# A transformer trunk in fp32: a written engine order for the mixing stages, and the sibling's order behind mixing and in the last output

## The chip, the cores and the metric

The kernel runs on one core of one Trainium2 chip. A core has TensorE (PE, with its weight loads shown apart as PEld), VectorE (DVE), ScalarE (ACT), GpSimd (POOL) and SyncE (SP), each with an instruction queue of its own that it works off in order; 16 DMA engines move data, on requests that here come from SP and POOL. The metric is device time in microseconds (us) of one execution, the median of several.

## The reference, cut to what matters

Two layers over 512 tokens of width 1024. Each layer is a half-step SwiGLU feed-forward, a mixing step, and a second feed-forward; each is preceded by an RMS norm with a scale and shift made from `c`.

```python
for l in range(DEPTH):
    mod = (c_act @ w_ada[l] + b_ada[l]).reshape(B, N_MOD, D_MODEL)
    hn = rms_norm(h, g_ffn1[l]) * (1.0 + sc1) + sh1
    h = h + 0.5 * (1.0 + gt1) * swiglu(hn, w_ffn1_in[l], w_ffn1_out[l])
    hn = rms_norm(h, g_mix[l]) * (1.0 + sc2) + sh2
    proj = hn @ w_mix_in[l]
    y_att = sliding_window_sink_attention(p_att, ...)   # 8 heads of 64, window 128
    y_rwkv = rwkv7_time_mix(p_rwkv, ...)                # 4 heads of 64, a recurrence over time
    y_conv = short_conv_mix(p_conv, conv_w[l])
    h = h + (1.0 + gt2) * (concatenate([y_att, y_rwkv, y_conv]) @ w_mix_out[l])
    hn = rms_norm(h, g_ffn2[l]) * (1.0 + sc3) + sh3
    h = h + 0.5 * (1.0 + gt3) * swiglu(hn, w_ffn2_in[l], w_ffn2_out[l])
```

## The kernel before

Activations lie transposed, 128 channels on the partitions and 512 tokens along the free axis. Large products are made in float32 accuracy from three products of reduced words: ScalarE casts a weight tile to its high half `wH` (`split`, L145), VectorE subtracts it to get the low half `wL` (L147), and `mm3` (L133 to L135) issues high x high, high x low and low x high. Weight tiles of 128 x 1024 arrive in `wraw` (two buffers); `wH` and `wL` have four buffers each. The feed-forwards make part of their products by a Strassen scheme with fewer block products (`prod`, L440 to L442, sums of weights by accumulating DMAs and by VectorE).

PSUM banks go by four tags, `mm`, `r0`, `r1` and `x`, two buffers each. `psmm` turns through the tags it is given with a counter, `turn`.

*Norms.* `norm` gives five steps. While the last two output tiles (6 and 7) of a stage are still being made in halves of 256 tokens, `stats` sums the squares over channels with tiny products into `ps_ss` (L279), takes root and reciprocal, `spread` turns the result across partitions by PE, and `apply` writes the normed `hn` as high and low parts (L296 to L298). The squares of tiles 0 to 6 are added on VectorE into `ss` (L255); that of tile 7, and of tile 6 in mixing, goes to `stats` apart.

*Projections.* `projector` makes the tiles of a stage's first product. Where it begins on its own, the first three tiles are made side by side in halves of the tokens, so that PE can start when the first half of `hn` is there; further tiles follow one by one, each with the next weights fetched ahead.

*Mixing* (`mix`). Twenty projection tiles feed three coroutines: `rwkv` (the recurrence in chunks of 64, many small products in 64 x 64 tiles), `attention` (scores, softmax, transposes `ps_pt`, averages `ps_av`) and `inverse` (a triangular inverse on VectorE that goes twice through DRAM on POOL's queue). A loop places their steps between the large products with a hand-kept clock (`STEP`, `PACE`, `DELAYS`, `WAITS`, `HALFWAY`). Order edges hold a step behind the large product ahead of it (`pe`, L808 to L814) and a few pairs of instructions apart. Beyond those edges a scheduler orders each engine's instructions when the program is built; on the chip the order on each engine is fixed. Names that the text uses: `lo`, `ps_w`, `ps_a` (decay and rate from a low-rank product), `rn`, `rk`, `rs` (sums for roots, 32 tiny products each), `ps_vt` (turn of the values `vr`), `ps_q`, `ps_rq` (norm of the queries), `ps_c`, `ps_x`, `ps_t`, `ps_gn`, `ps_o`, `ps_s`, `ps_ys` (the recurrence), `yr` (its result). Then six output tiles, and tiles 6 and 7 in halves.

*The last output* (`strassen_out`). The last feed-forward's second group has no norm behind it. For u = 0 and 1 it makes four output tiles each by products into `ps_d`, `ps_f`, `ps_g`; for u = 0, `rest_rows` also makes the part of all eight tiles that does not fit the scheme, through tag `x`, with its own weight tile each four.

Of the kernel before, what the change touches and what calls it, by code (L numbers as in the profile page):

```python
# [17 lines left out]
P = 128  # L18
# [30 lines left out]
WAITS = (5, 5, 4)  # L49
HALFWAY = (2.5, 2.5)  # L50
LOG = False


# [21 lines left out]
def trunk_kernel(ctx, tc, ins, out, layers=L, phases=("ffn1", "mix", "ffn2")):  # L75
# [52 lines left out]

    def mm3(acc, w, k, x, sl, start, stop):

        wH, wL, xH, xL = w[0][:, k], w[1][:, k], weave(x[0][:, sl]), weave(x[1][:, sl])
        acc = paired(acc)
        mm(acc, wH, xH, start=start, stop=False)  # L133
        mm(acc, wH, xL, start=False, stop=False)  # L134
        latest["large"] = mm(acc, wL, xH, start=False, stop=stop)  # L135

    latest = {}

    def queue_behind(name):
        return tc.issue_after(latest[name].ins) if name in latest else nullcontext()  # L140

# [105 lines left out]
    def add_ss(ss, i, sl=ALL):  # L247

        if ss is None:
            return  # L250
        if i == 0:
            act(ss[:, sl], h[0][:, sl], AF.Square)
        else:
            sq = square(i, sl)
            latest["dve"] = tt(ss[:, sl], ss[:, sl], sq, ALU.add)  # L255

# [5 lines left out]
    def norm(l, g, ish, isc, ss):  # L262

        hn = [tuple(hnp[k // 4].tile([P, T], F32R, name=n, tag="hn") for n in ("hnH", "hnL")) for k in range(KD)]
        gm = small_.tile([P, KD], F32, name="gmod", tag="gmod")
        rstd = {}

        def scale(ks=slice(0, KD)):
            stt(gm[:, ks], mod[l, isc][:, ks], 1.0, prm(l, g)[:, ks], ALU.add, ALU.mult)

        def stats(sl, sqs):

            pt = psum([P, 2], "ps_ss")
# [8 lines left out]
            latest["dve"] = nc.vector.reciprocal(r, r)  # L282
            rstd[sl.start] = r

        def spread(sl):

            r, pt = rstd[sl.start], psum([P, T // 2], "ps_rstd", "r0" if sl.start else "x")
            for b in range(2):
                mm(pt[:, b * P : (b + 1) * P], r[:, b : b + 1].to_broadcast([P, P]), cst("ident"), start=True, stop=True, is_transpose=True)
            rstd[sl.start] = pt  # L290

        def apply(sl, ks=range(KD)):
            for i in ks:
                a, b, sh = hn[i][0][:, sl], hn[i][1][:, sl], mod[l, ish][:, i : i + 1]
# [3 lines left out]
                latest["dve"] = latest["norm_dve"] = stt(b, t, sh, a.bitcast(F32), ALU.add, ALU.subtract)  # L298

        return hn, scale, stats, spread, apply  # L300


    loads = []

# [9 lines left out]
    def projector(srcs, hn, tags, pts=None, ahead=0, ready=(), first=("mm", "mm", "r1")):  # L314


        ws = list(ready) if pts is None else [None] * len(pts) + list(ready)

        def fetch(n):

            places = {3: ("norm_act", "norm_dve"), 4: ("act", "dve")} if ready and pts is None else {}
            ws.extend(load_w(s, behind=places.get(len(ws))) for s in srcs[len(ws) : n])

        if pts is None:
            fetch(3)
            pts = [psum([P, T], "ps_mm", tag) for tag in first]
            for sl in HALVES:
                for k in range(KD):
                    for w, pt in zip(ws, pts):
                        mm3(pt[:, sl], w, k, hn[k], sl, k == 0 and sl is HALVES[0], k == KD - 1 and sl is HALVES[1])  # L330
                    yield
            whole = [Woven(pt, 2) for pt in pts]
        else:
            whole = [Woven(pt) for pt in pts]
        n0 = len(pts)
        fetch(n0 + ahead)
        yield from whole
        for n in range(n0, len(srcs)):
            fetch(n + 1 + ahead)
            w = ws[n]  # L340
            pt = psmm(tags)
            for k in range(KD):
                mm3(pt, w, k, hn[k], ALL, k == 0, k == KD - 1)
                yield
            yield Woven(pt)

    def residual(pt, i, gate, ss, sl=ALL):
        hs = inorder(h[i][:, sl])
        done = stt(hs, Woven(pt).view, gate[:, i : i + 1], hs, ALU.mult, ALU.add)  # L349
        add_ss(ss, i, sl)  # L350
        return done
# [6 lines left out]
    def ffn(l, w_in, w_pair, w_out, hn, im, ss, need, then, first, ready, coming):  # L358
# [6 lines left out]
        with tc.tile_pool(name="act", bufs=1) as ap_:  # L365
# [10 lines left out]
            def hl(w, add_to=None):  # L376
                pair = tuple(wp.tile([P, KD, P], F32R, name=x, tag=x, bufs=4) for x in ("wH", "wL"))
                parted = split(*pair, w)
# [148 lines left out]
            def strassen_out(j0, j1):  # L527
# [37 lines left out]

                def rest_rows(u):
                    w = hl(raw_([(slice(2 * i, 2 * i + 2), w_out[l, 4 * u + i, :, kc:j1]) for i in range(4)]))
# [5 lines left out]
                    return classical  # L573

                for u in range(2):
                    tags = ("mm", "r0", "r1") if u else ("mm", "r1", "r0")
# [175 lines left out]

    def mix(l, hn, ss, mp, then, ready):
        wi, wo1, wo2 = ins["wmi"], ins["wmo1"], ins["wmo2"]

# [52 lines left out]
        def pe(*args, **kw):  # L808

            m = mm(*args, **kw)  # L810
            if lead[0] is not None:
                tc.add_manual_dep(m.ins, lead[0].ins.name, ORDER, reason="a step stands behind the large products before it")
                lead[0] = None
            return m  # L814
# [242 lines left out]
        def rwkv():  # L1057
# [91 lines left out]
            def invert():  # L1149
# [8 lines left out]
                for lev in range(2):  # L1158
# [7 lines left out]
                    for later in held if lev else ():  # L1166
                        tc.add_manual_dep(later.ins, new.ins.name, ORDER, reason="the inverse goes first")
                    yield 1.4, 3.2
# [165 lines left out]
        def attention():  # L1334
# [44 lines left out]
            def together(m, other, kind=ORDER):  # L1379

                if other is not None:
                    tc.add_manual_dep(m.ins, other.ins.name, kind, reason="both groups run together")

# [13 lines left out]
            for b in range(NB):  # L1397
# [4 lines left out]
                for g, (Sc, (den, es)) in enumerate(zip(both, dens)):  # L1402
# [4 lines left out]
                    for later in turns if (b, g) == (2, 0) else ():  # L1407
                        tc.add_manual_dep(later.ins, share.ins.name, ORDER, reason="shares go first")
                    yield 0, 1.4
# [73 lines left out]
        spread(HALVES[1])  # L1483
        apply(HALVES[1])


    what = {"ffn1": ("g1", 0), "mix": ("gm", 3), "ffn2": ("g2", 6)}
# [171 lines left out]
    for n, (l, p) in enumerate(seq):  # L1659
# [111 lines left out]
```

## Time and profile before

| | |
|---|---|
| median of 3 runs | 1773.5 us (1771.95 to 1773.51) |
| profiled execution | 1774.42 us |
| its span, first to last instruction | 1772.7 us |
| first mixing stage | from about 358 to 572 us |
| second mixing stage | from about 1231 to 1447 us |
| last output | from about 1718 us |

The page gives busy time, instructions and share of the span of each engine. In the timeline a row has the start, the length from first start to last end, engine, line, operation, names and shape; in brackets the idle time of the engine before it and what ended that. Successive matmuls overlap in the drawing: their ends are modelled, so the distance of their starts tells the pace.

### The profile page before, as it was taken

Reading aid. Unit: us, or ns where it says so; the run is one execution under the profiler, and the core shown is the slowest. Engines: PE = TensorE matmul, PEld = TensorE weight load, DVE = VectorE, ACT = ScalarE, POOL = GpSimd, SP = SyncE. Lnnn points to the kernel's source line nnn. Section 1 sums busy time; section 2 is a strip of 40 time slices with the busy share of each in tenths; the row PEclk is TensorE's granted clock in tenths of the full one; section 3 lists DMA queues with packets and bytes.
Section 4 is the critical chain, followed back from the end, with each engine's and each line's share of the span. In section 5 each row is a group of like instructions: output and inputs, shape, how many; then the busy total and the mean of one; then the engine's idle time right before and its main releaser. Section 6 shows DMA issues by size and latency. Waiting matters only on the chain.

```text
span 1772.7 us, 35390 instructions
## 1 busy us (share of the span) xinstructions
PE 1754.2 (99%) x14624; PEld 1594.7 (90%) x14624; DVE 1383.3 (78%) x2224; ACT 857.1 (48%) x1336; POOL 148.5 (8%) x233
## 2 busy tenths in 40 slices
PE   9999999999999999999999999999999999999998
PEld 7898999987778999899899989999777789999998
DVE  7877687877868887677888776877696788864897
ACT  7452365364444553255355514544645355533653
POOL 0101101101000011110100020110100000010000
PEclk9999999999999999999999999999999999999999
DMA  9667877623133676877737687773321428684764
GB/s 379 220 184 256 224 199 213 200 81 100 43 125 101 196 187 215 256 204 206 242 112 197 173 295 202 199 228 123 114 67 50 143 76 231 170 243 127 201 178 109
DMA packets 95442, 313.18 MB, mean 177 GB/s; under 512 B 10864, under 2 KB 13168, under 8 KB 94256
## 3 DMA queue, kind: packets, MB, share of 16 engines
q1 hardware_dynamic: 65088, 203.68, 34.3%
q0 software_dynamic: 30192, 107.23, 24.6%
q8 instruction: 115, 1.88, 0.4%
q14 instruction: 47, 0.39, 0.1%
HBM read 306.93 MB, written 3.93 MB: 175 GB/s over the span
## 4 chain that ended last, share of the span: by engine, by line
PE 82%; DVE 8%; ACT 4%; DMA 3%; issue 2%; POOL 0%; SPq 0%; DVEq 0%; ACTq 0%; POOLq 0%
PE ps_mm L133 13%; PE ps_mm L135 13%; PE ps_mm L134 13%; PE ps_d L440 7%; PE ps_d L441 7%; PE ps_d L442 7%; PE ps_f L442 3%; PE ps_f L441 3%; PE ps_f L440 3%; DMA wada<-in_wadaT 2%; PE ps_mm L1586 2%; DVE wL L147 2%; PE ps_g L441 2%; PE ps_g L442 2%; PE ps_g L440 2%
## 5 line engine op out<-in xcount | busy, mean ns | idle before, releaser
L145 ACT CAST wH<-wraw 128x1024 fp32r<-128x1024 f32 (+2 forms) x273 | 251.7, 927 | 431.7 <-PE ps_mm L134 195.3
L147 DVE TENSOR_TENSOR wL<-wraw,wH 128x1024 fp32r<-128x1024 f32 (+2 forms) x273 | 291.3, 1071 | 109.8 <-ACT wH L145 109.1
L133 PE MATMUL ps_mm<-actH,wH 128*128 128x512 f32 (+1 forms) x700 | 253.7, 362 | 1.2 <-DVE h L349 1.2
L135 PE MATMUL ps_mm<-actH,wL 128*128 128x512 f32 (+1 forms) x700 | 253.0, 361 | 0.3 <-DVE wL L147 0.3
L134 PE MATMUL ps_mm<-actL,wH 128*128 128x512 f32 (+1 forms) x700 | 252.9, 361 | 0.0
L133 PE MATMUL ps_mm<-hnH,wH 128*128 128x512 f32 (+1 forms) x712 | 249.3, 356 | 1.4 <-ACT wH L145 0.8
L134 PE MATMUL ps_mm<-hnL,wH 128*128 128x512 f32 (+1 forms) x712 | 244.8, 346 | 0.2
L135 PE MATMUL ps_mm<-hnH,wL 128*128 128x512 f32 (+1 forms) x712 | 244.4, 345 | 0.6 <-DVE wL L147 0.6
L440 PE MATMUL ps_d<-comH,wH 128*128 128x256 f32 x864 | 238.5, 276 | 0.0
L441 PE MATMUL ps_d<-comL,wH 128*128 128x256 f32 x864 | 237.6, 275 | 0.0
L442 PE MATMUL ps_d<-comH,wL 128*128 128x256 f32 x864 | 237.6, 275 | 0.0
L147 DVE TENSOR_TENSOR wL<-sum,wH 128x1024 fp32r<-128x1024 f32 x110 | 134.5, 1224 | 78.7 <-ACT wH L145 78.3
L204 DVE SCALAR_TENSOR_TENSOR wada<-wada,crep 128x1024 f32<-128x1024 f32 x128 | 153.2, 1219 | 39.7 <-DMA wada<-in_wadaT 39.5
L145 ACT CAST wH<-sum 128x1024 fp32r<-128x1024 f32 x110 | 115.0, 1047 | 118.9 <-PE ps_f L441 39.4
L440 PEld LDWEIGHTS ps_d<-comH,wH 128*128 128x128 f32 x864 | 165.8, 192 | 1.7 <-ACT s L466 1.6
L442 PEld LDWEIGHTS ps_d<-comH,wL 128*128 128x128 f32 x864 | 165.9, 192 | 0.0
L441 PEld LDWEIGHTS ps_d<-comL,wH 128*128 128x128 f32 x864 | 165.9, 192 | 0.0
L133 PEld LDWEIGHTS ps_mm<-hnH,wH 128*128 128x128 f32 x712 | 133.1, 190 | 25.6 <-issue 9.7
L133 PEld LDWEIGHTS ps_mm<-actH,wH 128*128 128x128 f32 x700 | 132.6, 189 | 17.5 <-DVE h L349 2.1
L135 PEld LDWEIGHTS ps_mm<-hnH,wL 128*128 128x128 f32 x712 | 135.2, 190 | 14.0 <-DVE wL L147 1.0
L135 PEld LDWEIGHTS ps_mm<-actH,wL 128*128 128x128 f32 x700 | 132.7, 190 | 16.3 <-DVE wL L147 0.9
L134 PEld LDWEIGHTS ps_mm<-actL,wH 128*128 128x128 f32 x700 | 132.7, 190 | 15.5 <-DVE actL L446 0.2
(428 smaller groups left out, 3971.6 us busy)
## 6 DMA issues: line engine op xcount, KB each, us to landing
wada<-in_wadaT POOLq DMA_DIRECT2D x126, 512.0 KB, 5.0
wraw<-in_wmi SPq DMA_DIRECT2D x40, 512.0 KB, 3.7
wraw<-in_w2p SPq DMA_DIRECT2D x36, 512.0 KB, 4.6
wraw<-in_w1p SPq DMA_DIRECT2D x32, 512.0 KB, 4.5
wraw<-in_w1o SPq DMA_DIRECT2D x32, 384.0 KB, 4.8
wraw<-in_w2o SPq DMA_DIRECT2D x32, 384.0 KB, 4.1
wraw<-in_w1o SPq DMA_DIRECT2D x32, 320.0 KB, 3.9
sum<-in_w2p SPq DMA_DIRECT2D x18, 512.0 KB, 4.4
```

The lines of the kernel that those rows point to most:

```text
L133: mm(acc, wH, xH, start=start, stop=False)
L134: mm(acc, wH, xL, start=False, stop=False)
L135: latest["large"] = mm(acc, wL, xH, start=False, stop=stop)
L145: latest["cast"] = nc.scalar.copy(hi, src)
L147: return nc.vector.tensor_sub(lo, src, hi.bitcast(F32))
L204: stt(w, w, 1.0, crep, ALU.mult, ALU.mult, accum_out=out_)
L440: mm(acc, wH, xH, start=start and i + k == 0, stop=False, skip_group_check=True)
L441: mm(acc, wH, xL, start=False, stop=False, skip_group_check=True)
L442: mm(acc, wL, xH, start=False, stop=k == 3, skip_group_check=True)
L1586: latest["large"] = pin("PE", mm(paired(pts[n]), w, x, start=first, stop=last, skip_group_check=True))
```

## The change

1. *Mixing.* While `mix` is traced, the order edges that it made by hand are left out (`free_order`, `loose`). At the end `kept_order` takes, for each of the two layers, a table of instruction numbers per engine, counted in program order from the layer's first mixing instruction, and chains all of them with order edges. The tables reach from the last products of the stage before (negative numbers) to the first ones of the stage behind.
2. *Tile order.* In `projector`, where it begins on its own, the first product of each further tile gets an order edge to the last large product traced before it; the bank counter `turn` is reset after the first three tiles. Where no weights were made ready by the stage before (behind mixing), the low half of the second weight tile is queued on VectorE behind the last `ss` addition and that of the third behind one of the norm's low parts (`AHEAD`).
3. *Norms.* The square of tile 5 is not added into `ss`; it goes to `stats` as a further operand. `rstd` gets a small tile of its own in place of a work buffer.
4. *Last output.* `rest_rows` takes its banks from `x`, `mm`, `x`, `r1` in turn; its weights are requested ahead; for u = 0 the cast of `S` comes ahead of `last_part`, which is queued behind that split; for u = 1 the addition to `S` comes ahead of the `s1` rows.

```diff
+TURN = 1
+AHEAD = {1: (None, "ss"), 2: (None, ("low", 0, 2))}
+FREE = True
+MIX = ({
+    "PE": """
+-58+2 -68+8 -56 -60 -55+4 -59 -51+18 -26+8 -33+3 3 0 -30+4 4+3 12 1 7 2 9 8 15+2 13+2 10+2 17 21 18+3 24+3 22+2 27+10 42 39+3 48+2 37+2 -18+16 50 45+3
...
+111+2 108+2 113+2 148 115+2 123 110 117 149 118 124 120+2 119 126+2 150 128 135+3 125 132+3 141 122 129+3 138+3 142+2 151+14 173+9 167+2 165 172 169
+166 171 170 188+32 182+6 220+4 236+4 224+6 240+8 230+2 256+12 284+3 232+3 248+2 268+16 252+4 250+2 235 287+16 312+3 303+3 315+9 306+6 324+2 327 326
...
+    "DVE": """
...
+    "Activation": """
...
-    def mm3(acc, w, k, x, sl, start, stop):
+    def mm3(acc, w, k, x, sl, start, stop, follow=None):
...
-        mm(acc, wH, xH, start=start, stop=False)
+        lead = mm(acc, wH, xH, start=start, stop=False)
+        if follow is not None:
+            loose(lead.ins, follow.ins.name, ORDER, reason="tiles keep their order")
...
+    def loose(later, name, kind, reason):
+        if not free_order[0]:
+            tc.add_manual_dep(later, name, kind, reason=reason)
...
-        return tc.issue_after(latest[name].ins) if name in latest else nullcontext()
+        return tc.issue_after(latest[name].ins) if name in latest and not free_order[0] else nullcontext()
...
         def stats(sl, sqs):
+            sqs = [fifth[0][:, sl]] + sqs
...
-            r = E("rstd")[:, :2]
+            r = small_.tile([P, 2], F32, name="rstd", tag="rstd")
...
-            places = {3: ("norm_act", "norm_dve"), 4: ("act", "dve")} if ready and pts is None else {}
+            places = {} if pts is not None else {3: ("norm_act", "norm_dve"), 4: ("act", "dve")} if ready else AHEAD
...
             whole = [Woven(pt, 2) for pt in pts]
+            turn[0] = TURN
...
-                mm3(pt, w, k, hn[k], ALL, k == 0, k == KD - 1)
+                mm3(pt, w, k, hn[k], ALL, k == 0, k == KD - 1, None if k or not inorder_ else latest["large"])
...
-        add_ss(ss, i, sl)
+        if ss is not None and i == 5:
+            fifth[0] = square(5, sl)
+        else:
+            add_ss(ss, i, sl)
...
-                        pt = psum([P, T], "ps_mm", "x")
+                        pt = psum([P, T], "ps_mm", ("x", "mm", "x", "r1")[i])
...
+                left_ = [rest(0)]
...
-                        rest_rows(0)
-                        classical = rest_rows(1)
-                    with tc.issue_after(classical.ins) if classical else nullcontext():
-                        tt(flat(s1), vG, flat(s1), ALU.add)
-                        rows_to(4 * u, cg, lo_, s1)
+                        left_.append(rest(1))
+                        rest_rows(0, left_[0])
+                        classical = rest_rows(1, left_[1])
+                    if not u:
+                        with tc.issue_after(classical.ins):
+                            tt(flat(s1), vG, flat(s1), ALU.add)
+                            rows_to(4 * u, cg, lo_, s1)
...
-                    tt(S, S, a12, ALU.add)
+                    summed = tt(S, S, a12, ALU.add)
+                    if u:
+                        with tc.issue_after(summed.ins):
+                            tt(flat(s1), vG, flat(s1), ALU.add)
+                            rows_to(4 * u, cg, lo_, s1)
...
+                    wS = hl(S)
                     if not u:
-                        with tc.issue_after(classical.ins):
+                        with queue_behind("hl"):
                             last_part()
-                    prod(pF, hl(S), B22, False)
+                    prod(pF, wS, B22, False)
...
     def mix(l, hn, ss, mp, then, ready):
+        free_order[0] = FREE
+        bases.append(len(nc.inst_names()))
...
+    def kept_order(bases):
...
+        for base, table in zip(bases, MIX):
+            for engine, runs in table.items():
+                mine = [n for n in names if str(of[n].engine).split(".")[-1] == engine]
...
+                for x, y in zip(seq, seq[1:]):
+                    tc.add_manual_dep(of[y], x, ORDER, reason="the mixing stage keeps its order")
...
+    kept_order(bases)
```

More of the change, by code (lines that the diff above doesn't have):

```diff
@@ L50 @@
 HALFWAY = (2.5, 2.5)
+TURN = 1
+AHEAD = {1: (None, "ss"), 2: (None, ("low", 0, 2))}
 LOG = False
+FREE = True
+MIX = ({
+    "PE": """
[23 rows of a table added]
+""",
+    "DVE": """
[9 rows of a table added]
+""",
+    "Activation": """
[5 rows of a table added]
+""",
+    "Pool": """
+9+2 5+2 0+5 7+2 12+4 11 16+2
+""",
+    "SP": """
+0 3+4 24 7+17 25+4 31+4
+""",
+}, {
+    "PE": """
[20 rows of a table added]
+""",
+    "DVE": """
[10 rows of a table added]
+""",
+    "Activation": """
[5 rows of a table added]
+""",
+    "Pool": """
+9+2 5+2 0+5 7+2 12+4 11 16+2
+""",
+    "SP": """
+0 3+4 24 7+17 25+4 31+4
+""",
+})
 def _columns(spec):
@@ L254, in add_ss @@
             sq = square(i, sl)
-            latest["dve"] = tt(ss[:, sl], ss[:, sl], sq, ALU.add)
+            latest["dve"] = latest["ss"] = tt(ss[:, sl], ss[:, sl], sq, ALU.add)
     def square(i, sl):
@@ L279, in stats @@
                         mm(pt[s, b : b + 1], x[:, s], ones[:, :1], start=n == 0, stop=n == len(parts) - 1)
-            r = E("rstd")[:, :2]
+            r = small_.tile([P, 2], F32, name="rstd", tag="rstd")
             latest["act"] = act(r, pt, AF.Sqrt, bias=vals["eps"], scale=1.0 / D)
-            latest["dve"] = nc.vector.reciprocal(r, r)
+            latest["dve"] = latest["recip"] = nc.vector.reciprocal(r, r)
             rstd[sl.start] = r
@@ L297, in apply @@
                 latest["act"] = latest["norm_act"] = act(a, t, AF.Identity, bias=sh)
-                latest["dve"] = latest["norm_dve"] = stt(b, t, sh, a.bitcast(F32), ALU.add, ALU.subtract)
+                latest["dve"] = latest["norm_dve"] = latest["low", sl.start, i] = stt(b, t, sh, a.bitcast(F32), ALU.add, ALU.subtract)
         return hn, scale, stats, spread, apply
-    loads = []
+    loads, fifth = [], [None]
     def load_w(src, n=KD, raw=None, pair=None, behind=None, landed=None):
@@ L377, in hl @@
                 pair = tuple(wp.tile([P, KD, P], F32R, name=x, tag=x, bufs=4) for x in ("wH", "wL"))
-                parted = split(*pair, w)
+                parted = latest["hl"] = split(*pair, w)
                 if add_to is not None:
@@ L564, in rows_to, with rest_rows @@
                         stt(hs, x[:, i], gate[:, i0 + i : i0 + i + 1], hs, ALU.mult, ALU.add)
-                def rest_rows(u):
-                    w = hl(raw_([(slice(2 * i, 2 * i + 2), w_out[l, 4 * u + i, :, kc:j1]) for i in range(4)]))
+                def rest_rows(u, src):
+                    w = hl(src)
                     for i in range(4):
-                        pt = psum([P, T], "ps_mm", "x")
+                        pt = psum([P, T], "ps_mm", ("x", "mm", "x", "r1")[i])
                         for k in range(2):
@@ L573, in rest_rows, with rest @@
                     return classical
+                def rest(u):
+                    return raw_([(slice(2 * i, 2 * i + 2), w_out[l, 4 * u + i, :, kc:j1]) for i in range(4)])
+                left_ = [rest(0)]
                 for u in range(2):
@@ L811, in pe @@
             if lead[0] is not None:
-                tc.add_manual_dep(m.ins, lead[0].ins.name, ORDER, reason="a step stands behind the large products before it")
+                loose(m.ins, lead[0].ins.name, ORDER, reason="a step stands behind the large products before it")
                 lead[0] = None
@@ L1166, in invert @@
                     for later in held if lev else ():
-                        tc.add_manual_dep(later.ins, new.ins.name, ORDER, reason="the inverse goes first")
+                        loose(later.ins, new.ins.name, ORDER, reason="the inverse goes first")
                     yield 1.4, 3.2
@@ L1381, in together @@
                 if other is not None:
-                    tc.add_manual_dep(m.ins, other.ins.name, kind, reason="both groups run together")
+                    loose(m.ins, other.ins.name, kind, reason="both groups run together")
             def turned(b, Sc):
@@ L1407, in attention @@
                     for later in turns if (b, g) == (2, 0) else ():
-                        tc.add_manual_dep(later.ins, share.ins.name, ORDER, reason="shares go first")
+                        loose(later.ins, share.ins.name, ORDER, reason="shares go first")
                     yield 0, 1.4
@@ L1484, in mix @@
         apply(HALVES[1])
+        free_order[0] = False
+    def kept_order(bases):
+        names = nc.inst_names()
+        of = {n: nc.get_inst_by_name(n) for n in names}
+        for base, table in zip(bases, MIX):
+            for engine, runs in table.items():
+                mine = [n for n in names if str(of[n].engine).split(".")[-1] == engine]
+                start = sum(str(of[n].engine).split(".")[-1] == engine for n in names[:base])
+                seq = []
+                for run in runs.split():
+                    a, _, n = run.partition("+")
+                    seq += [mine[start + int(a) + k] for k in range(int(n or 1))]
+                for x, y in zip(seq, seq[1:]):
+                    tc.add_manual_dep(of[y], x, ORDER, reason="the mixing stage keeps its order")
     what = {"ffn1": ("g1", 0), "mix": ("gm", 3), "ffn2": ("g2", 6)}
```

3 lines of the change are left out of this document (2 added, 1 removed), and 69 rows, old and new, of the table MIX.

## The prediction

> **What bounds the kernel now.** I read the page first, then the windows by stage, the waits of TensorE (PE) in the mixing stages, and the timeline around single waits.
>
> ```profile
> span 1772.7 us, 35390 instructions
> PE 1754.2 (99%) x14624; PEld 1594.7 (90%) x14624; DVE 1383.3 (78%) x2224; ACT 857.1 (48%) x1336; POOL 148.5 (8%) x233
> ...
> 358.00:572.00 214.00, 210.48 (x2459) 170.48 (x2458) 166.44 (x390) 110.54 (x239) 9.85 (x16) 1.00 0.28 90
> ...
> 600.00:880.00 280.00, 279.99 (x2026) 265.73 (x2025) 218.13 (x284) 129.48 (x169) 31.11 (x49) 1.00 0.74 218
> ...
> 1231.00:1447.00 216.00, 211.65 (x2469) 171.63 (x2469) 166.77 (x395) 110.52 (x238) 10.04 (x16) 1.00 0.29 89
> 1700.00:1773.00 73.00, 67.33 (x545) 64.38 (x543) 61.17 (x78) 31.25 (x39) 5.17 (x6) 1.00 0.52 139
> ```
>
> The window rows give stretch, length, then busy time of PE, PEld, DVE, ACT and POOL. PE is the bound everywhere, at full clock (1.00). A feed-forward stretch (600 to 880) has no idle PE; each mixing stage (358 to 572 and 1231 to 1447) has about 4 us of it, the last 73 us have 5.7 including the start of the output. So whatever an order can give is in mixing, just behind it, and in the tail. The waits of PE there (us, times, longest), first for layer 0 (345 to 575), then layer 1 (1232 to 1447), just behind it (1447 to 1465) and the tail (1715 to 1773):
>
> ```profile
> PE ps_vt L810 <- ACT vr L901: 1.7, 1, 1.7
> PE ps_rq L810 <- ACT qsq L935: 0.6, 1, 0.6
> PE ps_mm L133 <- ACT yrH L145: 0.3, 1, 0.3
> PE ps_t L810 <- DVE X L1165: 0.3, 1, 0.3
> PE ps_w L810 <- ACT lo L889: 0.2, 1, 0.2
> PE ps_mm L134 <- DVE y4L L147: 0.2, 1, 0.2
> PE ps_mm L133 <- ACT conv_c L961: 0.2, 1, 0.2
> ...
> PE ps_mm L133 <- ACT wH L145: 0.5, 1, 0.5
> PE ps_c L810 <- DVE AR L1206: 0.4, 1, 0.4
> ...
> PE ps_mm L135 <- DVE wL L147: 0.6, 1, 0.6
> PE ps_mm L133 <- ACT wH L145: 0.4, 1, 0.4
> ...
> PE ps_mm L133 <- DVE h L349: 1.2, 2, 0.7
> ```
>
> Layer 1 repeats the seven waits of layer 0 and adds the two rows shown after them. Idle is not all that is lost, since a small group has a price of its own beside the large products:
>
> ```profile
> 516.87 0.38 PE L134 MATMUL ps_mm<-y1L,wH 128*128 128x512 f32 x1
> 517.09 0.38 PE L135 MATMUL ps_mm<-y1H,wL 128*128 128x512 f32 x1
> 517.40 0.45 PE L810 MATMUL ps_s<-St,GT 64*64 64x64 f32 x8
> 517.77 0.48 PE L133 MATMUL ps_mm<-y2H,wH 128*128 128x512 f32 x1
> 518.10 0.38 PE L134 MATMUL ps_mm<-y2L,wH 128*128 128x512 f32 x1
> ...
> 398.50 1.16 PE L810 MATMUL ps_c<-AR,a 64*64 64x64 f32 x64
> 399.59 0.48 PE L133 MATMUL ps_mm<-hnH,wH 128*128 128x512 f32 x1
> ```
>
> Read the starts, not the durations. Large products of 512 columns start 0.22 us apart (516.87, 517.09), though each is drawn 0.38 long. Ahead of the group in 64x64 tiles the gap is 0.31, after it 0.33: 0.09 and 0.11 lost. The eight small ones take 0.37 us (517.40 to 517.77); 64 of that size take 1.09, so eight should take 0.14, and up to 0.23 more is the change of shape. One visit to tiled products costs 0.20 to 0.43 us; I take the middle, 0.32. The same picture says that a wait costs its idle and 0.16 us more, because idle is counted from the end of a product drawn 0.38 long whose follower could have started after 0.22.
>
> All sums are made on the profiled execution: span 1772.7 us, 1774.42 us with what lies around it, 0.9 over the median 1773.5.
>
> **The change, part by part.**
>
> *Fewer visits (PE's table).* I followed the indices to the matmuls that they count. Before, PE leaves the full 128x128 shape for a tiled one 39 times in layer 0 and 40 in layer 1; the table has 32 and 33, since it puts groups side by side (in layer 0 `165 172 ... 188+32`: the eight of `ps_w`/`ps_a`, then the 32 of `rn`). Three changes from one tiled shape to another are new per layer, each up to 0.23. Per layer 7 x 0.32 less 3 x 0.15 is 1.8; both layers **3.7 us** (bounds 2 x (7 x 0.20 - 3 x 0.23) = 1.4 and 2 x 7 x 0.43 = 6.0). The Trainium skill, "TensorEngine Tiling (Array Packing)", Key Properties, says that a change of mode, not of tile, drains TensorE; by it the three new changes would cost as much as visits, and this term would be 2 x 4 x 0.32 = 2.6.
>
> *The three waits on ScalarE at the front.* `ps_w` stands seven large products (1.5 us) later in the table, against a wait of 0.2. `ps_vt` follows the end of its tile by 3.2 us of large products in place of 1.7, and `vr` comes ahead of the two `iP` and one `P` exponentials in ScalarE's table. For `ps_rq`:
>
> ```profile
> 412.07 1.20 ACT L1200 COPY AX<-ps_ta 128x256 f32<-128x256 f32 x4 [1.21 <-PE ps_q L810]
> 413.13 0.72 ACT L935 ACTIVATE qsq<-ps_q,v_eps 128x512 f32<-128x512 f32 x1
> 413.87 1.28 ACT L942 ACT_TABLE_LOAD   x1
> ```
>
> The root of `ps_q` now stands behind four copies of 1.20 us; the table puts it ahead of them, more than the wait of 0.6. Three waits of 1.7 + 0.6 + 0.2 and 3 x 0.16 are 3.0 per layer, 6.0 for both; I leave 0.3 each for `ps_vt`, whose slack is a bare 3.2 against a need of 3.4 or so: **5.4 us** (bounds 0, if the waits only move, and 6.0).
>
> *The other waits in mixing.* Layer 0 has 0.3 + 0.3 + 0.2 + 0.2, layer 1 the same and 0.5 + 0.4: 2.9 idle in ten waits, 4.5 with 0.16 each. For `X` to `ps_t` the large products between the two are the same 3.3 us, only `ps_pt` moves; for `yrH` the second half of `ps_g` is put in the way of PE. I can't follow each: half, **2.2 us** (bounds 0 and 4.5).
>
> *Tile order behind mixing (`follow`, `TURN`, `AHEAD`).* The two waits just behind layer 1's mixing stand at the fourth tile: PE starts the fifth tile's weights before the fourth's, in layer 1 alone. The rows:
>
> ```profile
> 1458.71 0.28 PE L135 MATMUL ps_mm<-hnH,wL 128*128 128x256 f32 x1
> 1459.34 0.48 PE L133 MATMUL ps_mm<-hnH,wH 128*128 128x512 f32 x1 [0.35 <-ACT wH L145]
> 1459.66 0.38 PE L134 MATMUL ps_mm<-hnL,wH 128*128 128x512 f32 x1
> 1460.60 0.48 PE L135 MATMUL ps_mm<-hnH,wL 128*128 128x512 f32 x1 [0.56 <-DVE wL L147]
> ```
>
> 1458.71 to 1459.34 is 0.63 for a pitch of 0.11, 1459.66 to 1460.60 is 0.94 for 0.22: 1.2, and 0.1 for each product that restarts. With tiles in order and the bank turn reset, the weights used are those already split: **1.4 us** (bounds 0 and 1.4). The edge itself adds no wait: it binds PE to a PE instruction. `AHEAD` puts two low-half splits behind named VectorE work; queued behind them are the `hn` rows, which have the next tile's 1.2 us as cover.
>
> *Tail (`rest_rows`, `rest`, sums ahead of rows).* Before, eight outputs share the two `x` banks, and PE waits 1.2 in two waits for `h` at L349; four banks in turn free it. Restart and drawn ends make 1.7. VectorE is 61.17 of 73.00 busy there, so part returns later: **1.3 us** (bounds -0.5, if the casts for `rest` crowd out those of the sums, and 2.5, if the two small stalls on `wL` go too). The loads of `rest` are issued two ahead on SP, past `a11` and `S`; the stretch has its DMA engines half idle (0.52).
>
> *Fifth square.* Five adds leave VectorE (row below); 80 tiny matmuls join PE, 8 for each half of five norms:
>
> ```profile
> L255 DVE TENSOR_TENSOR ss<-ss,sq 128x512 f32<-128x512 f32 (+1 forms) x31 | 19.7, 634 | 4.2 <-ACT sq L259 4.2
> ```
>
> The adds are covered by PE: 0. The matmuls cost at most 80 x 0.017 (64 in 1.09) = 1.4 us; half, **-0.7**. `rstd` in a pool of its own pays for the slot that the square holds: 0.
>
> *New costs of the tables.* ScalarE's order goes root, exponential, root, exponential where it went root, exponential: two more function loads per layer at the 1.28 of the row above, four in all. ScalarE has 103 us idle in 214, so most hides: **-0.8** (bounds 0 and -5.1). The Trainium skill, "ScalarE: Activation LUTs", What ACT_TABLE_LOAD costs, charges a drain too, 2.66 us a switch; by it the four come to 10.6 of ScalarE; the row shows the load alone. New waits of an order that PE must keep, with the next large products queued behind the waiting one: I allow half a microsecond a layer, **-1.0** (bounds 0 and -8, all of today's idle again).
>
> Sum: 3.7 + 5.4 + 2.2 + 1.4 + 1.3 - 0.7 - 0.8 - 1.0 = 11.5 us. 1774.42 - 11.5 = 1762.9 on the profiled footing, **1762.0 us** as a median.
>
> **The rivals.**
>
> *The waits only move (same).* If chains on ScalarE and VectorE set the pace of mixing, PE arrives earlier and waits elsewhere. Left are half the visits, the tile order and the tail less the costs: 1.9 + 1.4 + 1.3 - 0.7 - 0.8 = 3.1, 1770.4. That the edges change little because the scheduler kept most of that order anyway gives the same. For it: most groups keep their place within a microsecond of large products. Against: the largest wait is order alone, and VectorE (166 of 214) and ScalarE (110) have room.
>
> *Function loads on the path (same).* If the four extra loads of 1.28 fall on PE in full and twice over, once ahead of an operand of PE and once ahead of the cast behind it, 10.2 goes in place of 0.8: 1762.0 + 9.4 = 1771.4. For it: two of PE's three front waits end on ScalarE just there. The trace shows no PE wait behind a load. The Trainium skill's page on activation tables, named above, has a price of this size.
>
> *Casts behind waiting work (slower).* Each layer has 33 weight casts (`wH`: 20 in, 10 out, 3 of the next stage) in ScalarE's fixed queue. If each comes late by d behind copies that wait for PE, PE loses 66 x d: the gain is gone at d = 0.17, and at 0.25 the kernel takes 1762.0 + 16.5 = 1778.5. For it: in the table several casts stand behind `beN`, `Sc` or `vN` copies. Against: four buffers, and the casts wait for PE to free one, not PE for casts, but for the two rows `wH` above.
>
> *All of it (faster still).* Every term at its upper bound, 6.0 + 6.0 + 4.5 + 1.4 + 2.5 less 0.7: 19.7, 1753.8.
>
> **How the numbers follow.** Forecast, 1755 to 1770: 0.73. Waits only move or loads on the path: 0.14. Casts late: 0.07. All of it: 0.06. A measurement of this kernel tells 0.2% (3.5 us) from no change: faster means below 1770.0, slower above 1777.0. Forecast and all of it are faster: 0.79; same 0.14; slower 0.07. The range 1754 to 1771.5 takes in the forecast with its unknowns and about half of the same case, 8 in 10.
>
> **What would show it.** Right: the waits of `ps_vt` and `ps_rq` gone or under 0.4 us; mixing windows some 4.5 us shorter each; the fourth tile ahead of the fifth behind layer 1's mixing with no wait on `wL`; no wait for `h` L349 in the tail. Wrong: new PE waits on `wH` or on a small product's operand in mixing that add up to over 4 us a layer, or feed-forward stretches longer than now because their order was disturbed.

## The result, and the profile after

The changed kernel takes 1757.82 us (median; the run before in the same session 1773.51). The ratio is 0.9912, with a 95% interval of 0.9898 to 0.9926. One of the six executions took 1793.04 us at a granted clock of 0.949; the ratio is made of the other five, 1757.24 to 1758.02. Forecast were 1762.0 us, 1754.0 to 1771.5. The profiled executions are 1774.42 before and 1757.24 after, 17.2 apart, of which 11.5 were forecast.

The page of the changed kernel (share of the span, and number of instructions):

```profile
span 1755.4 us, 35699 instructions
...
PE 1743.5 (99%) x14784; PEld 1595.6 (91%) x14784; DVE 1380.6 (79%) x2219; ACT 861.9 (49%) x1340; POOL 148.4 (8%) x233
```

There are 160 more records of matmuls, two for each of the 80 that the fifth square adds, and five fewer instructions on VectorE. TensorE (PE) is still busy 99%: 10.7 us of its busy time went, so the gain is not idle alone.

Windows don't show where, since everything behind a gain is shifted. A better clock is the work itself: both kernels run the same large products, 1596 us of them at their pitch, so I compare the moments at which both have started the same amount. Time gained between two such moments, on the profiled executions:

| place | us gained |
|---|---|
| ahead of the first mixing stage | -0.2 |
| first mixing stage | 7.3 |
| just behind it | -0.6 |
| feed-forwards between the mixing stages (the join near 890 us alone 1.0) | 0.8 |
| the join ahead of the second mixing stage | -0.25 |
| second mixing stage | 6.35 |
| just behind it | 1.45 |
| last output | 2.35 |

The sum is 17.2. The two mixing stages by kind, PE's matmuls taken by their starts:

| both stages | before | after |
|---|---|---|
| idle, us | 8.3 | 3.3 |
| large products beyond their pitch, us | 24.2 | 16.4 |
| small products, us | 109.5 | 108.7 |
| visits to tiled shapes | 39 + 41 | 31 + 34 |
| changes from one tiled shape to another | 7 + 7 | 10 + 10 |

So 5.0 us came from idle and 8.6 from large and small products that start closer together. The waits of PE that are left, first layer 0's mixing (340 to 575 us), then layer 1's with what lies behind it (1215 to 1470):

```profile
PE ps_pt L937 <- DVE Sc L1533: 0.8, 1, 0.8
...
PE ps_sc L937 <- DVE inv L1165: 0.9, 1, 0.9
PE ps_s L937 <- DVE St L1429: 0.8, 1, 0.8
PE ps_mm L235 <- ACT hnH L406: 0.7, 1, 0.7
```

None of the long waits of before is among them, and all four are new. The waits behind the second mixing stage are gone, and the same view of the last 65 us is empty. What removed the wait of `ps_rq` is seen in ScalarE's timeline of layer 0:

```profile
408.86 0.69 ACT L1062 ACTIVATE qsq<-ps_q,v_eps 128x512 f32<-128x512 f32 x1 [0.31 <-PE ps_q L937]
413.91 0.37 ACT L1327 COPY AX<-ps_ta 128x256 f32<-128x256 f32 x1 [4.36 <-PE ps_ta L937]
```

The root starts as soon as `ps_q` is there, with 0.31 us of idle ahead of it; the `AX` copies that stood ahead of it now follow 4.4 us later. One new wait shows a fixed queue at its worst (the join behind the second mixing stage):

```profile
1428.72 1.06 ACT L253 CAST wH<-wraw 128x1024 fp32r<-128x1024 f32 x1 [1.16 <-DMA wraw<-in_w2i]
...
1429.67 0.91 ACT L406 ACTIVATE hnH<-hn_t,mod 128x256 fp32r<-128x256 f32 x2
...
1430.24 0.38 PE L235 MATMUL ps_mm<-hnH,wH 128*128 128x256 f32 x1 [0.73 <-ACT hnH L406]
```

ScalarE waits 1.16 us for a weight load, in order to cast it; the `hnH` row that PE needs first is queued behind. This is the rival "casts behind waiting work", in one place. ScalarE's table of layer 1 ends with one `hnH` row behind the cast before; the next cast is not in it, and the scheduler put it ahead of that row.

### The profile page after: what moved, and what is told of

Read it like the earlier page. It is cut to its first block, busy times and chain, and to the rows that moved or that the text cites. A ratio compares the mean times of both kernels' runs of the same rounds, so it can differ in the third digit from the quotient of the medians.

```text
span 1755.4 us, 35699 instructions
## 1 busy us (share of the span) xinstructions
PE 1743.5 (99%) x14784; PEld 1595.6 (91%) x14784; DVE 1380.6 (79%) x2219; ACT 861.9 (49%) x1340; POOL 148.4 (8%) x233
## 5 line engine op out<-in xcount | busy, mean ns | idle before, releaser
L235 PE MATMUL ps_mm<-hnH,wH 128*128 128x512 f32 (+1 forms) x712 | 242.5, 352 | 0.7 <-ACT hnH L406 0.7
L239 PE MATMUL ps_mm<-hnH,wL 128*128 128x512 f32 (+1 forms) x712 | 240.6, 345 | 0.0
L238 PEld LDWEIGHTS ps_mm<-hnL,wH 128*128 128x128 f32 x712 | 134.1, 190 | 13.2 <-issue 1.3
```

The costliest lines, as they stand in the source:

```text
L235: lead = mm(acc, wH, xH, start=start, stop=False)
```

## The experiments

The times are medians where a ratio is given, else that of one execution; before took 1774.4, 1772.7, 1774.7 and 1773.1 in the four sessions (medians in the first and third, one execution each in the others). The table has the two mixing stages by the count above, against the changed kernel:

| run | time, us | more in layer 0, us | more in layer 1, us | idle, both | visits |
|---|---|---|---|---|---|
| before | 1773.5 | 7.3 | 6.35 | 8.3 | 39 + 41 |
| changed kernel | 1757.8 | 0 | 0 | 3.3 | 31 + 34 |
| no tables, edges by hand (e1) | 1771.2 | 7.9 | 7.3 | 9.5 | 37 + 40 |
| no tables, no edges (e2) | 1786.1 | 15.2 | 13.3 | 19.5 | 37 + 40 |
| PE's table alone (e3) | 1797.4 | 22.2 | 18.3 | 29.5 | 31 + 34 |
| all but PE's (e4) | 1787.4 | 10.7 | 18.7 | 12.0 | 43 + 49 |
| 42 visits, 30 tiled changes more (e5) | 1786.0 | 19.0 | 9.9 | 3.9 | 73 + 34 |
| all but ScalarE's (e6) | 1775.9 | 7.5 | 11.0 | 15.1 | 31 + 34 |
| all but VectorE's (e7) | 1806.4 | 23.5 | 26.2 | 32.8 | 32 + 34 |
| PE's table and the other engines' edges (e8) | 1796.3 | 20.9 | 18.1 | 27.5 | 31 + 34 |
| old ends (e9) | 1767.8 | -0.1 | 5.0 | 6.7 | 31 + 34 |
| long waits taken out (e10) | 1756.6 | -0.4 | -0.1 | 1.7 | 30 + 34 |
| more groups merged (e11) | 1760.3 | 0.0 | 2.2 | 3.8 | 28 + 31 |
| no reset of the bank counter, old last output (e12) | 1766.2 | -0.2 | 2.2 | 5.5 | 31 + 34 |

**Tables off, edges by hand back (e1).**

```diff
-FREE = True
+FREE = False
...
-    kept_order(bases)
```

> The changed kernel with its tables off and the hand-made order edges of mixing back; tile order, fifth square, rstd and tail stay. Theory (the written order makes the gain in mixing): the two mixing stages give back their 7.1 and 6.6 us, less the 0.6 lost behind the first; what stays is the tail (2.3), the tile order (1.4) and the join at 880 to 905 us (1.0). 1757.8 + 13.1 = 1770.9, between 1769.5 and 1772.5. Rival (the fifth square and the small rstd tile already shorten the mixing stages' ends): half of the 13.1 or more stays, 1764.5 or less.

1771.2 us, ratio to before 0.9985 (0.9975 to 0.9994). The theory holds: the mixing stages are back at 7.9 and 7.3 us more, with the waits of before, `ps_vt` at 1.7 again. By the medians the tables are worth 13 us and all the rest of the change about 3; the count by place is taken on this run's slowest execution (1773.54).

**Tables taken away by engine (e2, e3, e4, e6, e7).** For e2 `kept_order` alone is left out; for the others its loop skips engines:

```diff
             for engine, runs in table.items():
+                if engine != "PE":
+                    continue
```

> The hand-made order edges of mixing left out and no tables in their place: the scheduler alone. Theory (it takes a written order to put the tiled groups side by side): no gain over the hand-made edges, 1771 or more, and 39 or more visits of PE to tiled products per layer. Rival (the edges by hand were the cost, the tables only keep what the scheduler finds without them): 1758 to 1762.

> Of the tables only TensorE's. Theory (TensorE's order carries the gain; VectorE and ScalarE follow by what is ready): 31 and 34 visits as in the changed kernel, 1758 to 1760.5. Rival (ScalarE's order is needed for the front, the roots and vr ahead of the copies): the waits of ps_vt, ps_rq and ps_w come back, 2 x 2.5 of idle and 0.16 a wait: 1763 or more.

> Of the tables all but TensorE's. Theory (TensorE's order carries it): 38 visits or more per layer and TensorE's small groups placed as the scheduler likes; 1767 to 1772. Rival (ScalarE's and VectorE's order carries the waits, 8.3 us of idle in the two stages before): most of these waits stay gone without TensorE's table, 1761 to 1765.

> The tables without ScalarE's. The run with TensorE's table alone was 40 us slower than the changed kernel, so some other table is needed beside it. Theory (VectorE's order is what TensorE's table needs; ScalarE has room): 1758 to 1763, the new waits on vr and qsq only. Rival (ScalarE's order, the roots and vr ahead of the copies, is needed as well): waits of ps_vt, ps_rq and ps_w as before, 1765 or more.

> The tables without VectorE's. Theory (VectorE's order is what TensorE's table needs): near the run with TensorE's table alone, 1785 to 1800, with waits on X, Sc, r and y4L. Rival (ScalarE's order is the one missing there): 1758 to 1768.

e2 is slow as the theory had it (1771 or more); its 37 visits in layer 0 are fewer than the 39 expected, with 40 in layer 1. For e3 the theory is wrong by 37 us; the rival's bound holds, but not its reason. The kernel has the visits of the changed one, yet it is slower than before by 23. Its longest waits in layer 1 say why (then those of e7, without VectorE's table):

```profile
PE ps_mm L235 <- DVE r L930: 3.9, 1, 3.9
PE ps_t L937 <- DVE X L1292: 2.1, 1, 2.1
PE ps_v L937 <- ACT wide L982: 1.5, 1, 1.5
PE ps_vt L937 <- ACT vr L1028: 1.3, 1, 1.3
```

```profile
PE ps_pt L937 <- DVE Sc L1533: 6.5, 2, 6.3
PE ps_t L937 <- DVE X L1292: 3.1, 1, 3.1
PE ps_sc L937 <- DVE rq L1068: 2.4, 1, 2.4
```

PE keeps to its order and stands at the first product whose operand the other engine makes late: 29.5 and 32.8 us of idle. VectorE's table is the one missed most, with the waits that the theory named and 49 us lost, more than its 1785 to 1800 allowed; without ScalarE's (e6) 18 are lost and all of the gain with them, as the rival had it, not the 1758 to 1763 of the theory. Without PE's (e4) visits go up to 43 and 49 and idle to 12, and 1787.4 lies beyond what either side expected. A part of these losses is the clock: PE's mean granted clock is 0.996 in e3, 0.997 in e4 and 0.990 in e7, against 1.000 in the changed kernel. The missing shares of the spans are 7, 5 and 18 us, an estimate for a PE that always has work (see the last section). So no single table carries the gain. Each of the three is right only beside the others; the short ones of GpSimd and SyncE were not taken out alone.

**PE's table with the edges of the other engines (e8).** The two edge groups on VectorE ("the inverse goes first", "shares go first") and `queue_behind` stay on; only PE's table is used.

> TensorE's table alone, but with the hand-made order edges of VectorE and ScalarE back. Theory (each engine's order has to fit TensorE's new one; the old edges were made for the old order): waits on VectorE stay, slower than before, 1775 to 1797. Rival (the loss with TensorE's table alone came from the missing hand-made edges, since the run without any table and edge lost 15 us against the one with the edges): the edges bring those 15 us back and the table its gain, 1760 to 1770.

1796.3: the edges by hand bring back 1 of the 40 us. They were made for another order.

**The price of a visit, and of a change between tiled shapes (e5).** In PE's table of layer 0, 42 large products are moved back, one by one, into the middle of the tiled group behind them; in layer 1 two groups are interleaved. Shown with the program's names:

```diff
-ps_mm ps_mm ps_mm ps_c+36
+ps_c+9 ps_mm ps_c+9 ps_mm ps_c+9 ps_mm ps_c+9
...
-ps_vN+32 ps_kaN+16
+ps_vN+2 ps_kaN ps_vN+2 ps_kaN ...
```

> The changed kernel with two edits of TensorE's table, one per layer. Layer 0: one large product is put into the middle of a group of tiled products at 42 places, so 42 visits more. Theory (a visit costs the change of shape, 0.32 us): 13.4 us more in layer 0's mixing stage, 8.4 at the lower bound of 0.20 and 18.1 at the upper of 0.43, with little new idle. Rival (what the shorter mixing stages saved beside idle were restarts behind waits, a visit itself costs no more than the 0.1 on each side of it): 8.4 or less. Layer 1: the 32 products of ps_vN in 64x64 tiles and the 16 of ps_kaN in 64x128 tiles are interleaved two to one, so 30 changes more from one tiled shape to another. Row of the trace (0.14 a change): 4.2 us more in layer 1's mixing stage. If such a change costs as much as a visit, 9.6; if it is free, 0.

Layer 0: 19.0 us more, 0.5 of it idle, so 18.5 for 42 visits: **0.44 us each**, just above the upper bound of 0.43. The timeline of one group cut in this way:

```profile
429.94 0.48 PE L238 MATMUL ps_mm<-hnH,wH 128*128 128x512 f32 x1
430.35 0.89 PE L940 MATMUL ps_c<-AR,iP 64*64 64x128 f32 x22
431.17 0.48 PE L241 MATMUL ps_mm<-hnL,wH 128*128 128x512 f32 x1
431.58 0.87 PE L940 MATMUL ps_c<-AR,iP 64*64 64x128 f32 x20
```

By the starts, a large product alone between two groups holds PE for 0.41 us in place of its pitch of 0.22; the rest of the price is inside the groups. Layer 1: the interleaved stretch at full clock, then the same products in the changed kernel:

```profile
1335.76 0.33 PE L940 MATMUL ps_vN<-con,v 64*64 64x64 f32 x4
1336.02 0.27 PE L940 MATMUL ps_kaN<-con,iP 64*128 64x64 f32 x1
1336.22 0.33 PE L940 MATMUL ps_vN<-con,v 64*64 64x64 f32 x4
```

```profile
1315.34 1.16 PE L937 MATMUL ps_vN<-con,v 64*64 64x64 f32 x64
1316.43 0.71 PE L937 MATMUL ps_kaN<-con,iP 64*128 64x64 f32 x16
1317.08 0.65 PE L937 MATMUL ps_av<-pmc,V 128*64 128x512 f32 x2
```

A product of `ps_vN` has two records. A turn of two and one takes 0.46 us by the starts, sixteen of them 7.4; side by side the same takes 1.74. That is 5.7 us for 30 changes, **0.19 us each**, not the 0.14 of the row and not the price of a visit; a visit has two changes. The Trainium skill, "TensorEngine Tiling (Array Packing)", Key Properties, says that a change of mode drains TensorE: the trace fits it, since each change has a price near 0.2, whether the full shape is one of the two or not. The other 4 of the 9.9 us are a matter of the clock, below.

**The old ends (e9) and the bank counter (e12).**

```diff
-                mm3(pt, w, k, hn[k], ALL, k == 0, k == KD - 1, None if k or not inorder_ else latest["large"])
+                mm3(pt, w, k, hn[k], ALL, k == 0, k == KD - 1, None)
...
-            turn[0] = TURN
...
-        if ss is not None and i == 5:
+        if ss is not None and i == 5 and turned_.append(i) is None and len(turned_) != 3:
```

and the last output's lines as they were before. In e9 the low halves of `AHEAD` are not placed either. In e12 the reset of `turn` is left out, the last output is old, and the rest stays.

> The changed kernel with three of its parts undone, each in a place of its own: the last output as before; the tile order behind mixing as before (no edge, no reset of the bank counter, no placing of the two low-half splits); and the fifth square added on VectorE again at one join, that between the second feed-forward of layer 0 and the first of layer 1. Theory (each part makes the gain that the two traces show in its place): 2.3 us more in the tail, 1.4 more just behind layer 1's mixing, 1.0 more at the join at 880 to 900 us with PE's wait of 0.8 for the square back; together 4.8, 1762.0 to 1763.0. Rival for the join (the wait went because ScalarE's work there fell otherwise, not by the fifth square): 0 there. Rival for the tail (not the four banks but the weights asked for ahead): cannot be told apart here, both are undone. Rival for the tile order (the written order of mixing, which reaches into the next stage, removed those two waits): 0.5 or less there.

> The changed kernel without the reset of the bank counter behind the first three tiles, and with the last output as before; the edge between tiles, the placing of the low halves and the fifth square stay. The run with the old ends lost 2.1 us in a wait of PE for h ahead of layer 1's mixing and 2.8 in it, places that its edits were not meant for. Theory (without the reset the tiles take other PSUM banks, and the written order, made for the old banks, waits there): the wait for h at 1215 to 1220 us comes back at 2 us, and 4 to 5 us are lost by 1290 us; the two waits just behind layer 1's mixing stay gone, as the edge keeps the tiles in order. Rival (the missing edge or the placing of the low halves made that wait): no wait for h there, 0.5 or less lost. Tail alone: theory 2.3 more, with the two waits for h; rival (the run with the old ends lost 3.4 there by the old last output itself) 3.4, with a wait for actL of 0.9 as well.

e9 gives 1767.8, not 1762 to 1763; e12 1766.2. By place: just behind the second mixing stage e9 loses the 1.45 again, with the two waits of before, as the theory had it. At the join near 890 us 0.36 of the 1.0 comes back, with a wait for the square of 0.3 in place of 0.8: the fifth square makes a third of that gain; where the rest is from was not tried. The last output costs 2.6 in e12, where it stands nearly alone (2.35 were expected, with the two waits for `h`); in e9 it costs 3.8, with a wait of 0.9 for `actL` that is 0.2 in e12. And e9 loses 5 us in and ahead of the second mixing stage, where none of its edits was meant to act. e12 settles the first part of that. Its waits around that stage, the two longest:

```profile
PE ps_mm L235 <- ACT silu L762: 2.3, 1, 2.3
PE ps_mm L235 <- DVE h L459: 2.1, 1, 2.1
```

The wait for `h` is back with the reset of the counter alone taken away. `h` reads `ps_mm`, so PE waits for a PSUM bank: without the reset a tile of the projection falls on another bank, which the written order frees later (the bank itself is not in the trace). The wait in mixing (for `inv`, 1.1 here, 2.1 in e9) is not settled so: e12 loses 0.25 there, e9 2.8, so the missing edge or the placing of the low halves has part in it, and of the theory's 4 to 5 us by 1290 us only 2.3 came. The wait for `silu`, which also reads `ps_mm`, neither side expected: the edge keeps the fourth tile first, and without the reset its bank is not free; ScalarE does a cast and a function load of 1.28 us ahead of that `silu`. So the edge and the tables hold only with the reset that they were made with; the reset without the edge was not tried.

**Taking out the waits that are left (e10), and merging groups (e11).** Large products moved ahead of the waiting group in PE's tables, and in ScalarE's of layer 1

```diff
-200 175+2 201 177+7 202 184
+200 175+2 201 177+7 202 184+2 203
```

> The changed kernel with the four long waits that its trace still shows taken out of its tables. Layer 0: five large products go ahead of the group that waits 0.85 us for Sc, and the ps_sc behind it joins that group (a visit less). Layer 1: five large products go ahead of the group that waits 0.87 for inv, which joins the next ps_sc (a visit less); four large products go between the last two steps of the state, where PE waits 0.78 for St (a visit more); in ScalarE's table the two hnH rows come ahead of the cast that waits for its load, where PE waits 0.73 for hnH. Theory (a wait costs its idle and 0.16, a visit 0.44): 3.23 + 4 x 0.16 + 0.44 = 4.3 less, 1753.5. Rival (the chains on VectorE set the pace, the waits move to the next products): 1 or less, 1756.8 or more.

> The run before with five more pairs of groups put side by side, two in layer 0 (ps_sc with ps_sc, ps_xv with ps_sc) and three in layer 1 (ps_sc with ps_c, ps_xv with ps_sc, ps_o with ps_o). Theory (a visit costs 0.44): 2.2 less than the run before. Rival (longer stretches of small products pull the granted clock down, or a group that comes earlier or later waits): no better than the run before, or a stretch at clock 0.5 in the trace, and 1.7 us or more slower.

e10 takes 1756.6 us, ratio to before 0.9901 (0.9885 to 0.9918), not to be told from the changed kernel's 0.9912. What each edit gave, by the count of large products: the two `hnH` rows ahead of the cast 0.6 of their 0.73 + 0.16; `Sc` in layer 0 0.46 of 1.45; `inv` -0.2 of 1.5; the four products for `St` nothing, since they stand behind a later step than the one that waits. These come to 0.9, yet the profiled execution is only 0.1 shorter: 0.8 went again in the feed-forward near 1199 us, where PE waits 0.65 for a `wL` behind a late weight load and no edit stands. Its waits in layer 1:

```profile
PE ps_s L937 <- DVE St L1429: 0.7, 1, 0.7
PE ps_sc L937 <- DVE Sc L1484: 0.6, 1, 0.6
```

In place of `inv` PE waits for `Sc`, two products on. Here the rival, that waits move, is right. e11 has 28 and 31 visits, five fewer than e10, and is slower, not faster: 1760.3, with a new wait of 1.5 us for `conv_y` in layer 1. So a visit saved does not pay where the group or what stands behind it then waits; the granted clock stayed at 1.00 (the rival had it or a wait; it was the wait).

## Why the prediction was right, and where its sizes were off

The time lies in the range, and the mechanism was the forecast one: large waits at the front gone by order, fewer visits, ends repaired. Of its signs the waits named are gone, and the mixing stages are shorter by 7.3 and 6.35 us, not 4.5 each. The sum was 5.7 us short on the profiled execution. By its steps:

- *Fewer visits, 3.7.* Visits went from 39 to 31 and from 41 to 34, with three new tiled changes each, about as counted. At the measured prices that is 15 x 0.44 - 6 x 0.19 = **5.5**. The term was mis-sized: between 0.20 and 0.43 I took the middle, and the price is the upper end. The rows could have said so: the group of eight took 0.37 for work of 0.14, and no neighbour of it was idle.
- *The three front waits, 5.4.* All six waits are gone; their 5.0 of idle and 0.16 each make **6.0**. The 0.3 kept back for `ps_vt` was not needed.
- *The other waits, 2.2.* All ten are gone, not half: **4.5**.
- *New waits, -1.0.* There are five, with one of 0.1 for `gnsq`: 3.3 us of idle and 0.16 each, **-4.1**. These two terms were wrong by 2.3 and 3.1 the other way; together they came to 0.4 in place of 1.2.
- The four make 11.9, of 13.1 gained in mixing and just behind the first stage. The other 1.2 is left over, in products that start closer together; which, the runs did not separate.
- *Tile order, 1.4.* Measured **1.45**, and 1.45 lost again in e9. That the edge adds no wait holds only with the reset: e12 lost 4.2 there.
- *Tail, 1.3.* Measured **2.35** (2.6 in e12). The step that failed is "part returns later" on VectorE: no wait came back, and only one of 0.1 is left.
- *Fifth square, -0.7.* The tiny products cost the upper bound, not half of it: in the norms ahead of mixing, groups of 32, 8 and 24 products of `ps_ss` became 48, 16 and 32 and took, by the starts, 0.51, 0.24 and 0.36 us in place of 0.36, 0.17 and 0.30, so 0.28 a norm; the two joins there lost 0.2 and 0.25. Against it stands a gain that the forecast lacks: 1.0 near 890 us, 0.36 of it by the fifth square. The places ahead of the mixing stages and between them (-0.2, 0.8, -0.25) come to **+0.35**.
- *Function loads, -0.8.* ScalarE loads six times per mixing stage where it loaded four times, as forecast, and no wait of PE in the changed kernel ends on a load: **0** was seen. The Trainium skill's dearer price ("ScalarE: Activation LUTs", What ACT_TABLE_LOAD costs) is not seen either: a load takes 1.28 us, with under 0.03 of idle before the function behind it.

Of the rivals, "casts behind waiting work" came true in one place of 66, worth 0.9 us; "the waits only move" is what happened to e10, a second round of the same edit, not to the change; "all of it" (1753.8) missed by 4.0, the forecast by 4.2. What I did not see at all is how much the tables need each other: I priced PE's order and ScalarE's as separate terms, and e4, e6 and e7 show that any one of the three left out costs more than the whole gain.

## What to carry to other kernels

An order written for one engine is a claim on when the others deliver: write the engines' orders together, from one schedule, and with the buffers they were made for (one counter of banks undone cost 2 us in a place that its lines don't touch). Price a change of tile shape from an experiment that adds many of them, since the rows of one visit leave a factor of two. When the waits that an order could remove are gone, further edits move waits about: three waits of 2.4 us taken out gave 0.9 by place, and a time not to be told from the one before.

## What the runs showed of the hardware

In some runs the granted clock of PE is halved for some microseconds behind a wait of PE; neither before nor the changed kernel shows it during its work. In e12, behind the wait of 2.26 us for `silu`, and in e9, behind one of 2.1 us for `inv` (stretch, length, busy PE, PEld, DVE, ACT, POOL, clock, DMA share, GB/s):

```profile
1450.00:1454.00 4.00, 4.00 (x11) 3.23 (x12) 3.33 (x6) 2.93 (x4) 0.00 (x0) 0.57 0.92 306
1454.00:1458.00 4.00, 4.00 (x20) 3.52 (x19) 2.46 (x5) 0.06 (x1) 0.88 (x1) 1.00 1.04 377
```

```profile
1283.00:1287.00 4.00, 4.00 (x19) 2.72 (x17) 2.15 (x10) 2.76 (x6) 0.00 (x0) 0.58 0.27 105
```

A mean of 0.57 over 4 us is 3.4 us at half speed, so such a wait costs some 1.7 us beyond its own length. It is not sure to: e12's wait of 2.1 us for `h` was followed by full clock. The Trainium skill, "TensorE: Matmul & The Clock Gate", Part 1, has windows of 3.4 us and half speed after an idle one; the length agrees, though here waits of 2.1 and 2.3 us were enough. In e4 it lasted longer, behind a shorter wait: 1.62 us for `inv` at 1294, then 10 us at half clock, some 5 us of the 18.7 that e4 lost in layer 1:

```profile
1294.00:1304.00 10.00, 9.60 (x25) 7.03 (x26) 5.58 (x26) 0.00 (x0) 0.00 (x0) 0.51 0.19 54
```

The clock records of all runs have 20 such stretches of 3.4 to 10.2 us ahead of the end; 19 stand behind waits of 1.6 to 6.3 us. More surprising, PE need not wait at all. In e5, with PE drawn busy throughout:

```profile
1334.00:1338.00 4.00, 4.00 (x45) 2.82 (x42) 3.62 (x5) 0.00 (x0) 0.00 (x0) 1.00 0.00 0
1338.00:1348.00 10.00, 10.00 (x51) 5.13 (x52) 0.00 (x0) 2.58 (x8) 0.00 (x0) 0.50 0.19 54
```

Some four microseconds of tiny products, with two changes of shape in every three, were followed by 10 us at half clock, some 4 us of loss, nearly as much as the changes themselves. That the changes, not the size of the products, lowered the clock is argued only: the changed kernel runs the same products side by side at 1.00, but in 1.7 us. It was not tried apart.
